# A post-norm decoder trunk on one core: scale rows spread by TensorE at the start, and products grouped by high and low part

## The chip, the cores and the metric

One core of a Trainium2 chip runs the whole program. The time is device microseconds (us) of one execution; several executions are timed, and their median is given. A profile of one further execution shows every instruction on the engines: TensorE (PE, with its weight loads as PEld), the vector engine (DVE), ScalarE (ACT), GpSimd (POOL) and the queue engine (SP). ScalarE's and GpSimd's own DMA issues are shown as ACTq and POOLq.

## The reference

Two layers over 256 tokens of 1024 features, in float32, after one norm of the input (cut to what matters):

```python
h = _layer_norm(x, ln_in_g, ln_in_b)
for l in range(DEPTH):                                   # DEPTH = 2
    mix = _hybrid_mixer(h, positions, w_in[l], ...)      # three attention branches, gates, w_out
    h = _layer_norm(ALPHA * h + mix, ln1_g[l], ln1_b[l])
    ffn = _conv_gated_mlp(h, w_up[l], conv_w[l], conv_b[l], w_down[l])
    h = _layer_norm(ALPHA * h + ffn, ln2_g[l], ln2_b[l])

def _layer_norm(x, g, b):
    mu = jnp.mean(xf, axis=-1, keepdims=True)
    var = jnp.mean(jnp.square(xf - mu), axis=-1, keepdims=True)
    y = (xf - mu) * lax.rsqrt(var + LN_EPS) * g + b
```

The mixer begins with one projection of `h`, whose first 512 columns here are `bq`, the queries of the sparse branch. They are turned by rotary sines and cosines of the positions.

## The kernel before

The 256 tokens are two blocks of 128 (`tb` 0 and 1), one token on each partition. The residual `h` is four tiles of 128 x 512 (`h00`, `h01` for the first block, `h10`, `h11` for the second). A norm (`ln_tail`, `ln_apply`, `ln_stats`) takes statistics on the vector engine, computes the reciprocal deviation `rs` by a power on GpSimd, and applies scale and shift in four steps, two for each half: subtract the mean and multiply by the scale row, then multiply by `rs` and add the shift row. The scale row `lng` and the shift row `lnb` stand on all partitions, loaded as a broadcast. TensorE then transposes each half (four transposes of 128 x 128 into one PSUM bank), ScalarE copies the bank to a rounded high part `hTh`, and the vector engine subtracts to get the low part `hTl`.

Weights are split in the same way. The class `Stream` loads 512 KB chunks on the sync queue into seven buffers (`raw`), and `split` makes from each 128 x 512 item a high part (ScalarE) and a low part (vector engine, or GpSimd where `lo` says so), in 16 buffers `hl0`, `hl1`, and so on. A product of activations and weights is three TensorE instructions: high by high, low activations by high weights, high activations by low weights:

```python
    def mm3(o, lh, ll, rh, rl, start, stop):
        mm(o, lh, rh, start, False)
        mm(o, ll, rh, False, False)
        mm(o, lh, rl, False, stop)
```

A unit with 1024 input features and 512 columns has 8 k tiles, so 24 instructions for a token block. Behind a norm (`unit_x_tbfirst` for `bq` in each layer, and the first pair of the MLP) the first block's 24 go before the second's. The weight items `hl0` to `hl7` are those of `bq` in the first layer; `hl8` and on belong to the next unit, of 332 columns.

The order of every engine is written out as the program is built. Side work (norm tails, attention, rotary) lives in `Tasks` as generators; each `T.tick()` between the steps of the main products takes one step of each and may `refill` one weight split. `Clocks` keeps rough times of the engines, used only to decide that order. On the chip each engine runs its own list strictly in order.

The start of the program (from the comment `constants and first loads`, and again from `program`) sends the loads, normalizes the first block, then the second, and computes the rotary tables in `rotary_tables`: fifteen small operations on GpSimd (`posf`, `ang`, `rn`, `red`), then on ScalarE a load of the Sin table, sine `sn16`, cosine `cc16`, and a load of the table in use before, then copies on GpSimd.

Of the kernel before, what the change touches and what calls it, by code (L numbers as in the profile page):

```python
# [18 lines left out]
P = 128  # L19
D = 1024  # L20
# [14 lines left out]
# halves of the features before a norm  # L35
# [5 lines left out]
# columns of the constant array  # L41
# [32 lines left out]
def stream_plan():  # L74
    """Per layer: (name, first k tile, k tiles, columns) of each chunk in the order of use,
    and the pairs of the MLP whose down products follow a pair's up products."""
# [32 lines left out]
class Stream:  # L109
    """Weights: DMA of 512 KB chunks, each split into float32r high and low parts."""  # L110
# [62 lines left out]
    def refill(self, lo=None):  # L173
        """split one more item, unless the vector engine is behind and enough items are ready"""
# [12 lines left out]
class Clocks:  # L187
    """Rough times of the engines, kept while the program is written down: they only decide
    where in the engines' orders the side work is put."""
# [54 lines left out]
class Tasks:  # L244
    """Side work in pieces, put between the steps of the main products."""
# [40 lines left out]
def tile_hybrid(ctx: ExitStack, tc: tile.TileContext, a: dict, out: bass.AP):  # L286
# [71 lines left out]
    lng = hp.tile([P, D], F32, name="lng0", tag="lng")  # L358
    lnb = hp.tile([P, D], F32, name="lnb0", tag="lnb")
    ident = cpool.tile([P, P], F32, name="ident")  # L360
    sc.dma_start(ident, a["cst"][:, C_ID:C_ID + P])
# [4 lines left out]
    for q in range(2):  # L366
        bc_load(lng[:, 512 * q:512 * q + 512], a["ln_in_g"], 512, 512 * q, nc.sync)
        bc_load(lnb[:, 512 * q:512 * q + 512], a["ln_in_b"], 512, 512 * q, nc.sync)
    W.dma()
    W.dma()  # L370
    for q in range(2):
        nc.sync.dma_start(h[1][q], xv[:, 1, 512 * q:512 * q + 512])
    nc.sync.dma_start(cst[:, C_TRI:C_INVF], a["cst"][:, C_TRI:C_INVF])
    for _ in range(RAW_BUFS - 2):
        W.dma()
# [18 lines left out]
    mhalf = cpool.tile([P, 8], F32, name="mhalf")  # L394
    ve.memset(ones, 1.0)
# [7 lines left out]
    # rotary tables: cos|cos and -sin|sin for 16 and for 8 frequencies  # L403
# [10 lines left out]
    def rotary_tables():  # L414
        """sin and cos of the angles, reduced to [-pi, pi] in three steps"""
# [26 lines left out]
    def lambdas():  # L442
        """minus lambda of the differential attention, on every partition, and its scaled gains"""
# [22 lines left out]
    def ln_half(tb, q, st, bank=None, cols=(0, 512), slot=None):  # L466
        """residual of one half of the features (or a part of it), and its statistics"""
# [5 lines left out]
    def ln_stats(st):  # L473
        """mean and reciprocal deviation"""
# [6 lines left out]

    def ln_apply(tb, st, g, b):
        mu, rs = ln_stats(st)
        for q in range(2):
            y, gq, bq = h[tb][q], g[:, 512 * q:512 * q + 512], b[:, 512 * q:512 * q + 512]
            ve.scalar_tensor_tensor(y, y, mu, gq, ALU.subtract, ALU.mult)
            ve.scalar_tensor_tensor(y, y, rs, bq, ALU.mult, ALU.add)
# [12 lines left out]
    def last_norm0(st, g, b, half_done):  # L500
        """the last norm of the first tokens, spread over the engines"""
# [23 lines left out]
    def ln_tail(tb, st, hT, g, b, flag):  # L525
        """normalise, then transpose into hT"""
# [14 lines left out]
    def unit_x(lhs, kts, ncols):  # L541
        """out[tb] = [token, column]: x stationary, weights moving"""
# [10 lines left out]
    def unit_x_tbfirst(lhs, kts, ncols, ready=None):  # L553
        bk = [acc(), acc()]
        ws = []
        for tb in range(2):
            if ready is not None:
                T.until(lambda: tb in ready)
            for k in range(kts):
                if tb == 0:  # L560
                    ws.append(W.take())
                lh, ll = lhs(k, tb)
                mm3(bk[tb][:, :ncols], lh, ll, ws[k][:, 0, :ncols], ws[k][:, 1, :ncols], k == 0, k == kts - 1)
                if tb == 1:
                    W.free()
                T.tick()
# [708 lines left out]
```

## Time and profile before

| | |
|---|---|
| median of 3 runs | 938.44 us (937.15 to 938.46) |
| profiled execution, its own time: span from first to last instruction | 936.7 us |
| TensorE busy | 905.9 us (97%) |
| vector engine busy | 655.4 us (70%) |
| ScalarE busy | 514.3 us (55%) |
| GpSimd busy | 46.6 us (5%) |
| mean DMA rate | 172 GB/s |

The page gives the profiled execution by its span, which lies 1.74 us below the median of the runs. All instructions carry one line (L238, the recording helper), so the tiles' names tell them apart: `acc` and `att` are PSUM banks, `hl` is a split weight, `raw` a loaded one, `mv` mean and variance, `bst` the statistics, `kbT` the keys of one branch. In a row of the timeline `x2` stands for two instructions merged, and the time in brackets is the engine's idle time ahead of it.

### The profile page before, as it was taken

The page shows a single profiled execution, that of the slowest core. Times are in us where ns is not written, and L with a number is a line of the kernel's source. Part 1 is how long each engine was busy: PE and PEld are TensorE (multiplying, and loading weights), DVE is VectorE, ACT ScalarE, POOL GpSimd, SP SyncE. Part 2 cuts the span into 40 slices and gives each one's busy share as a digit, 9 for nine tenths or more (in the row PEclk, how much of TensorE's full clock was granted, in tenths as well). Part 3 has the DMA queues.
Part 4 walks back from the last instruction along what each step waited for, and adds up shares of the span by engine and source line. Part 5 has one row for each costly group of instructions (what it writes and reads, how often), then busy time and mean ns, then how long its engine had stood idle before and what let it go on. Part 6 is the DMA issues. An engine that isn't in the chain of part 4 may idle for free.

```text
span 936.7 us, 14398 instructions
## 1 busy us (share of the span) xinstructions
PE 905.9 (97%) x5306; PEld 791.9 (85%) x5306; DVE 655.4 (70%) x1270; ACT 514.3 (55%) x1008; POOL 46.6 (5%) x62
## 2 busy tenths in 40 slices
PE   4998999999999999999999999999999999999995
PEld 3876897888888999999988788888888799999994
DVE  6788657657668766666788975665667785766755
ACT  4665567555536655555456565765555375655541
POOL 5000010002000000000010000100110100000001
PEclk9999999999999999999999999999999999999998
DMA  8833427555535755565345343736665286565501
GB/s 305 274 118 113 135 91 260 188 200 185 180 132 211 240 186 191 169 197 191 115 155 174 115 147 111 255 112 206 190 196 179 76 305 200 176 193 192 177 8 45
DMA packets 46535, 161.45 MB, mean 172 GB/s; under 512 B 5696, under 2 KB 6208, under 8 KB 46464
## 3 DMA queue, kind: packets, MB, share of 16 engines
q1 hardware_dynamic: 44208, 154.94, 50.3%
q0 software_dynamic: 1408, 4.98, 1.7%
q8 instruction: 41, 0.67, 0.3%
q10 hardware_dynamic: 848, 0.60, 0.2%
q14 instruction: 30, 0.25, 0.1%
HBM read 159.46 MB, written 1.05 MB: 171 GB/s over the span
## 4 chain that ended last, share of the span: by engine, by line
PE 68%; issue 21%; DVE 7%; DMA 1%; POOL 1%; ACT 1%; SPq 0%; DVEq 0%; POOLq 0%; ACTq 0%
PE acc L238 48%; PE att L238 20%; DVE h L238 2%; DVE s L238 2%; DVE hl L238 1%; POOL rs L238 1%; DVE mx L238 1%; DMA raw<-in_w_dram 1%; DMA lnb<-in_ln_in_b_dram 1%; DVE bst L238 0%; DVE mv L238 0%; ACT h L238 0%; ACT p L238 0%; POOL hl L238 0%; DVE rv L238 0%
## 5 line engine op out<-in xcount | busy, mean ns | idle before, releaser
L238 DVE TENSOR_TENSOR hl<-raw,hl 128x512 fp32r<-128x512 f32 (+1 forms) x581 | 389.1, 695 | 189.6 <-ACT hl L238 188.1
L238 ACT ACTIVATE hl<-raw 128x512 fp32r<-128x512 f32 (+1 forms) x584 | 348.2, 624 | 192.0 <-PE att L238 94.6
L238 PE MATMUL acc<-hl,hTh 128*128 128x512 f32 (+1 forms) x896 | 287.8, 393 | 3.3 <-DVE hl L238 2.0
L238 PE MATMUL att<-hTh,hl 128*128 128x256 f32 x1280 | 231.5, 283 | 0.0
L238 PEld LDWEIGHTS att<-hTh,hl 128*128 128x128 f32 x1280 | 200.8, 192 | 1.4
L238 PEld LDWEIGHTS acc<-hl,hTh 128*128 128x128 f32 x896 | 168.9, 190 | 38.5 <-DVE hl L238 2.7
L238 PE MATMUL att<-hTl,hl 128*128 128x256 f32 x640 | 181.1, 283 | 0.0
L238 PE MATMUL acc<-hl,hTl 128*128 128x512 f32 (+1 forms) x448 | 174.1, 389 | 1.8 <-DVE hTl L238 1.8
L238 PE MATMUL acc<-hl,act 128*128 128x512 f32 x528 | 123.4, 390 | 0.0
L238 PEld LDWEIGHTS att<-hTl,hl 128*128 128x128 f32 x640 | 122.8, 192 | 0.0
L238 PEld LDWEIGHTS acc<-hl,act 128*128 128x128 f32 x528 | 97.9, 188 | 19.5
L238 PEld LDWEIGHTS acc<-hl,hTl 128*128 128x128 f32 x448 | 85.2, 190 | 17.8 <-DVE hTl L238 2.8
L238 PE MATMUL acc<-hl,oT 128*128 128x512 f32 x288 | 68.1, 391 | 0.0
L238 PEld LDWEIGHTS acc<-hl,oT 128*128 128x128 f32 x288 | 53.8, 188 | 11.0
L238 DVE SCALAR_TENSOR_TENSOR cv<-att,convp,cv 128x255 f32<-128x255 f32 x88 | 40.4, 480 | 15.6 <-ACT cv L238 14.0
L238 PE MATMUL acc<-hTh,hl 128*128 128x256 f32 x256 | 47.2, 286 | 0.0
L238 PE MATMUL acc<-hl,mT 128*128 128x512 f32 x192 | 45.4, 392 | 0.0
L238 ACT ACTIVATE hTh<-att 128x512 fp32r<-128x512 f32 x16 | 9.6, 598 | 58.9 <-PE att L238 58.9
L238 PEld LDWEIGHTS acc<-hl,mT 128*128 128x128 f32 x192 | 35.6, 188 | 7.1
L238 PEld LDWEIGHTS acc<-hTh,hl 128*128 128x128 f32 x256 | 39.9, 191 | 1.5 <-issue 1.3
L238 PE MATMUL acc<-hTl,hl 128*128 128x256 f32 x128 | 36.2, 283 | 0.0
L238 POOL TENSOR_TENSOR rs<-mv,mhalf 128x1 f32<-128x1 f32 x10 | 9.0, 904 | 482.2 <-DVE mv L238 482.2
(160 smaller groups left out, 696.0 us busy)
## 6 DMA issues: line engine op xcount, KB each, us to landing
raw<-in_w_dram SPq DMA_DIRECT2D x284, 512.0 KB, 4.3
raw<-in_w_dram SPq DMA_DIRECT2D x8, 332.0 KB, 4.1
lng<-in_ln_g_dram POOLq DMA_DIRECT2D x4, 512.0 KB, 4.2
lnb<-in_ln_b_dram POOLq DMA_DIRECT2D x4, 512.0 KB, 6.6
h<-in_x_dram SPq DMA_DIRECT2D x4, 256.0 KB, 4.6
lng<-in_ln_in_g_dram SPq DMA_DIRECT2D x2, 256.0 KB, 5.3
lnb<-in_ln_in_b_dram SPq DMA_DIRECT2D x2, 256.0 KB, 5.6
wu<-in_w_ukv_dram POOLq DMA_DIRECT2D x2, 256.0 KB, 3.0
```

What stands on the lines that cost most here:

```text
L238: f(*args, **kw)
```

## The change

1. The broadcasts of the first norm's scale and shift rows are gone. One row of 1024 each is loaded to one partition, first on ScalarE's queue, and four float32 products with a stationary row of ones spread the halves over all partitions, into two `acc` and two `att` banks, which the norm reads in place of `lng` and `lnb` until both blocks are through. Four bfloat16 products of a constant tile (`spin`) into a bank that is not read go ahead of them.
2. The first weight chunk is loaded ahead of the second block of `x`, and three more behind it.
3. `hl0` and `hl1` are split while the first block's norm is under way; after that five splits, with GpSimd taking the low parts of `hl2`, `hl3`, `hl4` and `hl6`. The rotary tables are started after these splits, where they had been started before the second block's norm.
4. Behind a norm, products go in groups of four k tiles: the four high by high, then the four with the low activations, then the four with the low weights (`mm3_group`). All ticks of a group fall into its last part. This holds for `bq` in both layers and for the first pair of the MLP in both.

The remaining lines of the diff only take away comments and pass `g` and `b` as two halves.

```diff
-    lng = hp.tile([P, D], F32, name="lng0", tag="lng")
-    lnb = hp.tile([P, D], F32, name="lnb0", tag="lnb")
     ident = cpool.tile([P, P], F32, name="ident")
+    gbr = [hp.tile([P, D], F32, name=f"{n}0", tag=n) for n in ("lng", "lnb")]
+    sc.dma_start(gbr[0][0:1, :], a["ln_in_g"].unsqueeze(0))
+    sc.dma_start(gbr[1][0:1, :], a["ln_in_b"].unsqueeze(0))
...
     for q in range(2):
         nc.sync.dma_start(h[0][q], xv[:, 0, 512 * q:512 * q + 512])
-    for q in range(2):
-        bc_load(lng[:, 512 * q:512 * q + 512], a["ln_in_g"], 512, 512 * q, nc.sync)
-        bc_load(lnb[:, 512 * q:512 * q + 512], a["ln_in_b"], 512, 512 * q, nc.sync)
-    W.dma()
     W.dma()
     for q in range(2):
         nc.sync.dma_start(h[1][q], xv[:, 1, 512 * q:512 * q + 512])
+    for _ in range(3):
+        W.dma()
     nc.sync.dma_start(cst[:, C_TRI:C_INVF], a["cst"][:, C_TRI:C_INVF])
-    for _ in range(RAW_BUFS - 2):
+    for _ in range(RAW_BUFS - 4):
         W.dma()
...
+    spin = t4([P, 512], BF16, n="spin")
+    ve.memset(spin, 1.0)
...
+    def mm3_group(o, ls, ws, first, last):
+
+        n = len(ls)
+        for i, (lh, ll) in enumerate(ls):
+            mm(o, lh, ws[i][0], first and i == 0, False)
+        for i, (lh, ll) in enumerate(ls):
+            mm(o, ll, ws[i][0], False, False)
+        for i, (lh, ll) in enumerate(ls):
+            mm(o, lh, ws[i][1], False, last and i == n - 1)
+            T.tick()
...
-            for k in range(kts):
+            for k in range(0, kts, 4):
                 if tb == 0:
-                    ws.append(W.take())
-                lh, ll = lhs(k, tb)
-                mm3(bk[tb][:, :ncols], lh, ll, ws[k][:, 0, :ncols], ws[k][:, 1, :ncols], k == 0, k == kts - 1)
+                    ws += [W.take() for _ in range(4)]
+                mm3_group(bk[tb][:, :ncols], [lhs(i, tb) for i in range(k, k + 4)],
+                          [(w[:, 0, :ncols], w[:, 1, :ncols]) for w in ws[k:k + 4]], k == 0, k + 4 == kts)
                 if tb == 1:
-                    W.free()
-                T.tick()
+                    W.free(4)
...
+    T.att += 3
+    idle = attp.tile([P, 512], F32, name=nm("att"), tag="att")
+    for _ in range(4):
+        mm(idle, spin[:, 0:P], spin, True)
+    gb = [[acc(), acc()], [attp.tile([P, 512], F32, name=nm("att"), tag="att") for _ in range(2)]]
+    for q in range(2):
+        for i in range(2):
+            mm(gb[q][i], ones[0:1, :], gbr[i][0:1, 512 * q:512 * q + 512], True)
+    T.att -= 1
+    gain, bias = [gb[q][0] for q in range(2)], [gb[q][1] for q in range(2)]
...
-    T.add(ln_tail(0, sts[0], hT, lng, lnb, hflag))
+    T.add(ln_tail(0, sts[0], hT, gain, bias, hflag))
     T.tick()
+    W.split()
+    W.split()
+    T.until(lambda: 0 in hflag)
+    for q in range(2):
+        ln_half(1, q, sts[1])
+    T.add(ln_tail(1, sts[1], hT, gain, bias, hflag))
+    W.low = LOW
+    for i in range(5):
+        W.refill((gp, gp, gp, ve, gp)[i])
+        T.tick()
     tables = rotary_tables()
     next(tables)
-    T.until(lambda: 0 in hflag)
-    for i in range(4):
-        W.refill(ve)
-    for q in range(2):
-        ln_half(1, q, sts[1])
-    T.add(ln_tail(1, sts[1], hT, lng, lnb, hflag))
-    W.low = LOW
-    for i in range(4):
-        W.refill((gp, gp, ve, gp)[i])
-        T.tick()
     T.add(tables)
```

The orders of three engines at the start, row by row. In a name the first number is the tile's own (`hl7` is the eighth weight item), the last a count of the program.

GpSimd, from the end of the rotary angles on. Before, all fifteen operations of the angles stand directly behind the first norm's power, and the first row here is their last:

```order
L238 TENSOR_TENSOR red_142<-red_142,rn_141 128x32
L238 TENSOR_TENSOR hl4_209<-raw2_115,hl4_209 128x512
L238 TENSOR_TENSOR rs_10_215<-mv_9_212,mhalf_135 128x1
L238 TENSOR_TENSOR hl5_221<-raw2_115,hl5_221 128x512
L238 TENSOR_TENSOR hl7_229<-raw3_117,hl7_229 128x512
```

After the change, from the first norm's power on:

```order
L238 TENSOR_TENSOR rs_12_169<-mv_11_166,mhalf_133 128x1
L238 TENSOR_TENSOR hl2_199<-raw1_110,hl2_199 128x512
L238 TENSOR_TENSOR rs_16_205<-mv_15_202,mhalf_133 128x1
L238 TENSOR_TENSOR hl3_211<-raw1_110,hl3_211 128x512
L238 TENSOR_TENSOR hl4_216<-raw2_112,hl4_216 128x512
L238 TENSOR_TENSOR hl6_224<-raw3_114,hl6_224 128x512
L238 CAST posf_139<-posi_95 128x2
L238 TENSOR_SCALAR ang_140<-cst_94,posf_139 128x16 x2
```

The fifteen operations of the angles have moved behind the second norm's power and three low parts.

ScalarE, around the Sin table (`ACT_TABLE_LOAD`). Before:

```order
L238 ACTIVATE hl6_226<-raw3_117 128x512
L238 ACTIVATE hl7_229<-raw3_117 128x512
L238 ACT_TABLE_LOAD
L238 ACTIVATE sn16_144<-ang_140 128x2x16
L238 ACTIVATE cc16_143<-red_142,half_pi_134 128x2x16
L238 ACT_TABLE_LOAD
L238 ACTIVATE hTh_1_147<-att_14_272 128x4x128
```

After the change:

```order
L238 ACTIVATE hl6_224<-raw3_114 128x512
L238 ACTIVATE hTh_7_160<-att_20_262 128x4x128
L238 ACTIVATE hTh_7_160<-att_21_269 128x4x128
L238 ACT_TABLE_LOAD
L238 ACTIVATE sn16_144<-ang_140 128x2x16
L238 ACTIVATE cc16_143<-red_142,half_pi_132 128x2x16
L238 ACT_TABLE_LOAD
L238 ACTIVATE hl7_286<-raw3_114 128x512
```

The second block's two `hTh` now stand ahead of the Sin, and `hl7`, the last item of `bq`, behind it.

TensorE, around the second block's transposes (`h10`, `h11`). Before, with 18 products of the first block ahead of the first row:

```order
L238 MATMUL att_14_272<-ident_98,h10_92 128x128 x4
L238 MATMUL acc_12_243<-hl6_226,hTh_1_147 128x512
L238 MATMUL acc_12_243<-hl6_226,hTl_2_148 128x512
L238 MATMUL acc_12_243<-hl6_226,hTh_1_147 128x512
L238 MATMUL att_15_285<-ident_98,h11_93 128x128 x4
L238 MATMUL acc_12_243<-hl7_229,hTh_1_147 128x512
```

After the change, with 8 products ahead of the first row:

```order
L238 MATMUL acc_18_251<-hl0_175,hTh_7_160 128x512
L238 MATMUL att_20_262<-ident_96,h10_92 128x128 x4
L238 MATMUL att_21_269<-ident_96,h11_93 128x128 x4
L238 MATMUL acc_18_251<-hl1_178,hTh_7_160 128x512
L238 MATMUL acc_18_251<-hl2_199,hTh_7_160 128x512
L238 MATMUL acc_18_251<-hl3_211,hTh_7_160 128x512
L238 MATMUL acc_18_251<-hl4_216,hTh_7_160 128x512
L238 MATMUL acc_18_251<-hl5_219,hTh_7_160 128x512
L238 MATMUL acc_18_251<-hl6_224,hTh_7_160 128x512
L238 MATMUL acc_18_251<-hl7_286,hTh_7_160 128x512
L238 MATMUL acc_18_251<-hl4_216,hTl_8_161 128x512
```

The transposes come after 9 of the first block's products, and `hl7` is used three instructions behind `hl4`, ahead of the low activations. At the three later norms both pairs of transposes come after 21 products; before, 18 came ahead of the first and 21 ahead of the second. Nothing else moves on TensorE.

## Rows read from the trace of the kernel before

**Rows 1.** The page, part 1: busy time, share of the span, instructions.

```profile
PE 905.9 (97%) x5306; PEld 791.9 (85%) x5306; DVE 655.4 (70%) x1270; ACT 514.3 (55%) x1008; POOL 46.6 (5%) x62
```

**Rows 2.** Busy time by stretch: PE, PEld, DVE, ACT, POOL, clock, DMA, GB/s.

```profile
0.00:24.00 24.00, 11.44 (x39) 8.00 (x40) 16.84 (x31) 11.01 (x18) 13.51 (x31) 1.00 0.82 299
24.00:48.00 24.00, 24.00 (x123) 21.03 (x122) 18.37 (x49) 16.11 (x37) 1.39 (x2) 0.93 0.78 266
48.00:140.00 92.00, 88.98 (x553) 75.80 (x552) 68.55 (x199) 51.19 (x138) 3.68 (x5) 1.00 0.35 115
```

**Rows 3.** Timeline (start us, duration us, instruction), vector engine, first block's norm.

```profile
3.66 1.32 DVE L238 BATCH_NORM_STATS2 bst<-h 128x6 f32<-128x512 f32 x2 [2.65 <-DMA h<-in_x_dram]
...
9.50 0.75 DVE L238 SCALAR_TENSOR_TENSOR h<-h,rs,lnb 128x512 f32<-128x512 f32 x1
```

**Rows 4.** Chain that ended last: start us, duration us, what.

```profile
2.10 5.79 DMA lnb<-in_ln_in_b_dram
```

**Rows 5.** Timeline, TensorE, first products.

```profile
12.62 0.80 PE L238 MATMUL acc<-hl,hTh 128*128 128x512 f32 x1 [1.21 <-ACT hl L238]
...
16.20 1.05 PE L238 MATMUL acc<-hl,hTh 128*128 128x512 f32 x2
...
17.48 0.64 PE L238 MATMUL acc<-hl,hTh 128*128 128x512 f32 x2
```

**Rows 6.** Timeline, TensorE, last transposes and end of the first projection.

```profile
23.18 0.60 PE L238 MATMUL att<-ident,h 128*128 128x128 f32 x4
...
30.48 0.61 PE L238 MATMUL acc<-hl,hTh 128*128 128x512 f32 x2
...
31.16 0.54 PE L238 MATMUL acc<-hl,hTh 128*128 128x512 f32 x2
```

**Rows 7.** DMA issues of the first 3.66 us: count, size, median us to landing.

```profile
h<-in_x_dram SPq DMA_DIRECT2D x2, 256.0 KB, 3.0
```

**Rows 8.** Timeline, TensorE, float32 products of another stage.

```profile
86.16 1.03 PE L238 MATMUL att<-kbT,t 128*128 128x256 f32 x4
87.02 0.38 PE L238 MATMUL att<-sb,negid 128*128 128x512 bf16 x1
```

**Rows 9.** The page, part 5: busy us, mean ns of one | idle before.

```profile
L238 DVE TENSOR_TENSOR hl<-raw,hl 128x512 fp32r<-128x512 f32 (+1 forms) x581 | 389.1, 695 | 189.6 <-ACT hl L238 188.1
L238 ACT ACTIVATE hl<-raw 128x512 fp32r<-128x512 f32 (+1 forms) x584 | 348.2, 624 | 192.0 <-PE att L238 94.6
```

**Rows 10.** Timeline, GpSimd: the powers, first and last operations of the angles.

```profile
5.49 0.55 POOL L238 TENSOR_TENSOR rs<-mv,mhalf 128x1 f32<-128x1 f32 x1 [5.06 <-DVE mv L238]
6.00 0.18 POOL L238 CAST posf<-posi 128x2 f32<-128x2 int32 x1
...
10.82 0.29 POOL L238 TENSOR_SCALAR red<-rn 128x32 f32<-128x32 f32 x1
...
12.46 0.25 POOL L238 TENSOR_TENSOR red<-red,rn 128x32 f32<-128x32 f32 x1
...
16.89 1.01 POOL L238 TENSOR_TENSOR rs<-mv,mhalf 128x1 f32<-128x1 f32 x1 [0.15 <-DVE mv L238]
```

**Rows 11.** Instructions on tile hl, 0 to 24 us: ns min/median/max, starts.

```profile
L238 POOL TENSOR_TENSOR hl<-raw,hl x3: 1277/1291/1733, 15.5 to 19.1; 128x512 fp32r<-128x512 f32 x3
```

**Rows 12.** Timeline, ScalarE, cosine and the table load behind it.

```profile
18.66 0.30 ACT L238 ACTIVATE cc<-red,half_pi 128x32 f32<-128x32 f32 x1
...
18.98 1.28 ACT L238 ACT_TABLE_LOAD   x1
...
20.46 0.60 ACT L238 ACTIVATE hTh<-att 128x512 fp32r<-128x512 f32 x1 [0.20 <-PE att L238]
```

**Rows 13.** Busy time by stretch, as in rows 2, inside the first projection.

```profile
24.34:27.75 3.41, 3.41 (x10) 2.65 (x9) 3.32 (x9) 3.41 (x10) 0.00 (x0) 0.50 0.77 197
```

**Rows 14.** Timeline, TensorE and vector engine, norm behind the first mixer.

```profile
283.75 0.50 PE L238 MATMUL acc<-hl,hTl 128*128 128x512 f32 x1 [0.61 <-DVE hTl L238]
...
288.61 0.75 DVE L238 SCALAR_TENSOR_TENSOR h<-h,rs,lnb 128x512 f32<-128x512 f32 x1
```

More of the change, by code (lines that the diff above doesn't have):

```diff
@@ L480, in ln_stats, with halves @@
         return mv[:, 0:1], rs
+    def halves(t):
+        return [t[:, 0:512], t[:, 512:1024]]
     def ln_apply(tb, st, g, b):
@@ L484, in ln_apply @@
         for q in range(2):
-            y, gq, bq = h[tb][q], g[:, 512 * q:512 * q + 512], b[:, 512 * q:512 * q + 512]
+            y, gq, bq = h[tb][q], g[q], b[q]
             ve.scalar_tensor_tensor(y, y, mu, gq, ALU.subtract, ALU.mult)
@@ L1065, in layer @@
                 ln_half(tb, nh, st, ob[nh][tb], (c0, c1), i)
-            T.add(ln_tail(tb, st, hT1, lng, lnb, flag1))
+            T.add(ln_tail(tb, st, hT1, halves(lng), halves(lnb), flag1))
         acts = {}
@@ L1084, in layer @@
             bk = acc()
-            for k in range(KD):
+            ts = slice(tb * P, (tb + 1) * P)
+            for k in range(0, KD, 4):
                 if tb == 0:
-                    ws.append(W.take())
-                ts = slice(tb * P, (tb + 1) * P)
-                mm3(bk, hT1[0][:, k, ts], hT1[1][:, k, ts], ws[k][:, 0, :], ws[k][:, 1, :], k == 0, k == KD - 1)
+                    ws += [W.take() for _ in range(4)]
+                mm3_group(bk, [(hT1[0][:, i, ts], hT1[1][:, i, ts]) for i in range(k, k + 4)],
+                          [(w[:, 0, :], w[:, 1, :]) for w in ws[k:k + 4]], k == 0, k + 4 == KD)
                 if tb:
-                    W.free()
-                T.tick()
+                    W.free(4)
             u = t2([P, 512], n="up0")
@@ L1178, in layer @@
             if l < DEPTH - 1:
-                T.add(ln_tail(tb, st, hT2, lng, lnb, flag2))
+                T.add(ln_tail(tb, st, hT2, halves(lng), halves(lnb), flag2))
             elif tb == 0:
@@ L1193, in tile_hybrid @@
     W.low = -1
-    T.add(ln_tail(0, sts[0], hT, lng, lnb, hflag))
+    T.add(ln_tail(0, sts[0], hT, gain, bias, hflag))
     T.tick()
+    W.split()
[8 more added lines that the diff above has]
+        T.tick()
     tables = rotary_tables()
     next(tables)
-    T.until(lambda: 0 in hflag)
-    for i in range(4):
-        W.refill(ve)
-    for q in range(2):
-        ln_half(1, q, sts[1])
-    T.add(ln_tail(1, sts[1], hT, lng, lnb, hflag))
-    W.low = LOW
-    for i in range(4):
-        W.refill((gp, gp, ve, gp)[i])
-        T.tick()
     T.add(tables)
@@ L1210, in tile_hybrid, with release_gb @@
     masks()
+    def release_gb():
+        while len(hflag) < 2:
+            yield
+        T.att -= 2
+    T.add(release_gb())
     def task_lambdas():
```

## The prediction

> **What bounds the kernel now.** I read the busy times first: TensorE works for 905.9 of 936.7 us [rows 1], so a change is worth what it adds to or takes from TensorE's 30.8 us of idle time and from its clock. The table by stages then says where the idle time lies: 12.6 us in the first 24 us, none from 24 to 48, 3.0 us between 48 and 140 [rows 2]. With no idle time behind it, whatever moves the end of the first projection (the 48 products of `bq`) moves the end of the program. That end is the figure I follow.
>
> The timeline of the start is a chain. The vector engine has the first tokens' statistics at 4.98 us and ends their norm at 10.25 [rows 3]; in between the chain of waits has 5.79 us of the load of `lnb`, issued at 2.10 [rows 4]. TensorE begins the products at 12.62 us; two cost 1.05 us at 16.20 and 0.64 at 17.48 [rows 5], so it begins at the lower of its two clocks. The last product of `bq` starts at 31.16 us; a product costs 0.227 us there, three in the 0.68 us from 30.48 [rows 6]. `bq` ends at 31.4 us.
>
> **First tokens' norm.** The 256 KB broadcasts go, and TensorE spreads two rows. The first loads of 256 KB land 3.0 us after their issue and are in use from 3.66 us [rows 3, 7]; the row of 4 KB goes out first on ScalarE's queue, and I take 3.3 us for its landing. The four spreads are float32: two float32 products of 256 columns go from 86.16 to 87.02 us, so one of 512 columns takes 0.86 us at full clock and 1.72 at half [rows 8]. All at full clock they end at 6.7 us, all at half at 10.2. The four `spin` products start at about 1.2 us, and TensorE needed the work from 12.62 to 17.48 us to get its full clock [rows 5]; 4.9 us after 1.2 is 6.1. By then 1.6 spreads are done, the other 2.4 take 2.0 us: 8.1 us. The norm's last step of 0.75 us stands behind the last spread: 8.1 + 0.1 + 0.75 = 8.95, against 10.25 [rows 3]. That gains 1.3 us, with bounds of a gain of 2.7 and a loss of 0.8.
>
> **The second tokens' norm** follows on the vector engine. Two low parts of weights now come ahead of the two of `hT` (four times 0.695 us [rows 9], 2.8 us), then the statistics, 1.32 [rows 3]: 13.1 us. GpSimd's power begins 0.51 us behind the statistics and takes 0.55 to 1.01 us [rows 3, 10]; I take its end at 14.2. Three more steps of 0.75 follow, and the last four transposes start at 16.4 and take 0.60 us: 17.0, where the trace has 23.18 for their start [rows 6]. So far this looks like a large gain.
>
> **What is moved behind it.** GpSimd computed the rotary angles from 6.00 to 12.71 us [rows 10], ahead of its three low parts. Now they stand behind all three and behind the second norm's power. ScalarE loads the Sin table, computes sine and cosine and loads the other table again, with the last weight tile of `bq`, `hl7`, queued behind; before, all eight tiles went ahead of the Sin. So `hl7` waits for GpSimd:
> - three low parts from 14.2 us, at the median of 1.29 us each: 18.1 us. The dearest was 1.73, which makes 1.3 us more for three [rows 11].
> - the angles: 6.71 us from first to last, part of it waiting for a constant and beside the norm. From 10.82 to 12.46 us five operations come 0.33 us apart [rows 10], which makes 5.0 us for all fifteen. The stretch ahead will be quieter than the first; I take 5.4: 23.5 us.
> - ScalarE: cosine 0.30 and table load 1.28 [rows 12], then the high part of `hl7`, 0.62 [rows 9]: 25.7 us. TensorE takes it at 25.8.
>
> The table load is a place to weigh. In the trace the load at 18.98 us takes 1.28, and the next activation starts at 20.46, after 0.20 us of waiting for TensorE [rows 12], so I use 1.28 alone. The Trainium skill (ScalarE: Activation LUTs, What ACT_TABLE_LOAD costs) puts a drain of about 1.38 us on top of every switch to a different set; by it the sum would come out 1.4 us later. The trace disagrees: 0.2 us is all that stands between that load and the next activation.
>
> **TensorE behind `hl7`.** In the new order the first block's second group asks for the high parts of `hl4` to `hl7` in a row. After 17.0 us six products are free to go (three with low weights, then `hl4`, `hl5`, `hl6`), 1.4 us at full clock and 2.7 at half; at 18.4 to 19.7 us TensorE stands, and waits until 25.8. Then 33 products remain, 9 of the first block and 24 of the second: 33 x 0.227 = 7.5 us. After six idle microseconds the clock will be down. The trace has 3.41 us at granted clock 0.50 in the middle of `bq` [rows 13], 1.7 us lost; the first start had 4.9 us at half [rows 5], 2.4 us lost. So long a stop is nearer to the first start, so 2.4. `bq` ends at 25.8 + 7.5 + 2.4 = 35.7 us instead of 31.4: **4.3 us later**.
>
> **The later norms** (three: after the first layer's mixer and MLP, after the second mixer). The new order fills the wait for `hTl`, 0.61 us at 283.75 [rows 14]. But 21 products stand ahead of the other block's last transposes, before as now, and those are released by the vector engine, whose order ahead of them is the same: its last step ends at 289.36 [rows 14]. TensorE arrives earlier and waits longer there; 27 products follow in both. I cost this edit at nothing, with the vector engine's norm as its cover; without that, three products a norm, 0.68 us, would come off, 2.0 in all.
>
> **Loads.** The sync queue loses 1 MB of broadcasts ahead of the weights, and seven raw buffers can fill while TensorE waits: zero. The smaller moves (a split later, four buffers freed at once) have 16 split buffers as cover: zero; if that cover went, it would be one split, 0.69 us, at each of four places.
>
> **Sum.** 936.7 + 4.3 = 941.0 us of span. The median of the runs stands 1.74 us above that span, so 938.44 + 4.3 = **942.7 us**. Ends of the unknowns: spreads all at full clock (-1.4), power 0.55 (-0.1), angles 5.0 (-0.4), clock loss 1.7 (-0.7) give +1.7; spreads all at half (+2.1), power 1.01 (+0.4), angles 6.7 (+1.3), dear low parts (+1.3) give +9.4, if all came together.
>
> **Rivals.**
> - **TensorE is not held (faster).** Were `hl7` there when TensorE comes, `bq` would end at 17.0 + 39 x 0.227 + 2.4 = 28.3 us, 3.1 us early: 935.3 us. It decides at about 19 us: the chain through GpSimd would have to be over 6 us shorter. For it: spans on GpSimd are rough, by the profile's own word. Against it: three low parts, the angles and the rest on ScalarE are 11.5 us behind a power that can hardly end before 13.
> - **The delay is absorbed (no change).** TensorE idles 3.0 us between 48 and 140 us [rows 2]. If what it waits for there did not move with `bq`, 3.0 of the 4.3 would vanish: 939.7 us. Against it: the selection and softmax it waits for work on these same projections.
> - **The later norms pay.** If the vector engine came 0.7 us earlier to those transposes, 2.0 us would come back: 940.7 us. Against it: nothing is taken from its queue ahead of them.
> - **A table switch costs a drain too**, 1.4 us before `hl7`: 944.1 us. The 0.2 us of [rows 12] speak against it. This is the rule of the page of the Trainium skill named above, ScalarE: Activation LUTs.
>
> **How the numbers follow.** Forecast 0.72, not held 0.08, absorbed 0.07, later norms 0.06, drain 0.07. A measurement of this kernel can tell about 0.2%, 1.9 us, from no change. Only the first rival is faster (0.08); the absorbed one is within 0.2% (0.07); the rest is slower (0.85). The range is 940.1 (+1.7) to 945.6 (+7.2, since the late ends will not all meet); it leaves out the first two rivals and a small tail of the forecast.
>
> **What would show it.** In the changed profile: four spreads of 0.9 to 1.7 us from about 3.3 us; the first tokens' last transposes near 9 us, the second's near 16.4; the angles on GpSimd from 18 to 23.5 us; one wait of TensorE of 6 to 7 us for ScalarE's `hl7`, ending near 25.8; a stretch at clock 0.50 around it; the first product of 332 columns near 35.7. At the later norms the wait for `hTl` gone and one of about 1 us for the vector engine in its place. I am wrong if `hl7` is ready before 20 us, if the angles end before 19 us, or if the waits between 48 and 140 us shrink by some 3 us.

## The result and the profile after

The changed kernel takes **945.37 us** (median of 4 runs, 944.97 to 946.11) against 938.45 us: a ratio of 1.0079 (95% interval 1.0067 to 1.0092), 6.9 us slower. Forecast were 942.7 us, 940.1 to 945.6. The direction and the mechanism are in the trace as forecast; the size is not. The median lies 0.2 us inside the upper end of the range; the ratio, applied to the 938.44 us that the forecast starts from, gives 945.9 us, just above it.

The page, part 1 (busy us, share, instructions), beside [rows 1]:

```profile
PE 914.2 (97%) x5318; PEld 794.5 (84%) x5318; DVE 655.0 (69%) x1270; ACT 514.9 (55%) x1008; POOL 45.7 (5%) x63
```

The span is 944.3 us, 7.6 more; TensorE's idle time has barely moved (30.1 us), its busy time has grown by 8.3. By stretch, with the columns of [rows 2]:

```profile
0.00:24.00 24.00, 16.77 (x43) 7.96 (x43) 15.70 (x30) 8.71 (x13) 9.77 (x21) 0.99 0.77 257
24.00:48.00 24.00, 20.38 (x97) 18.02 (x98) 13.87 (x27) 16.48 (x36) 2.77 (x12) 0.80 0.70 234
48.00:140.00 92.00, 88.96 (x527) 74.72 (x526) 70.09 (x209) 49.09 (x124) 1.91 (x3) 1.00 0.37 119
```

The start is busier because `spin` and the spreads count as work. The loss shows in the second row: 3.6 us idle where there was no idle time, and a granted clock of 0.80 for 0.93. (The same wait also fills the last 3.5 us of the first row.) The third row is as before, so nothing is absorbed there.

TensorE's timeline at the start, the rows that answer to [rows 5]; a float32 spread is two instructions here:

```profile
1.45 1.89 PE L238 MATMUL att<-spin 128*128 128x512 bf16 x4 [1.45 <-DVE spin L238]
3.27 2.07 PE L238 MATMUL acc<-lng,ones 1*128 1x512 f32 x2
...
8.55 1.91 PE L238 MATMUL att<-lnb,ones 1*128 1x512 f32 x2
...
12.19 1.22 PE L238 MATMUL acc<-hl,hTh 128*128 128x512 f32 x2
...
14.48 1.09 PE L238 MATMUL acc<-hl,hTl 128*128 128x512 f32 x4
15.40 0.39 PE L238 MATMUL acc<-hl,hTh 128*128 128x512 f32 x1
```

From 5.13 us the spreads start 1.71 us apart, the length at half clock in [rows 8]: all four run at the lower level, although TensorE has worked since 1.45. The products of the four low parts at 14.48 us (0.92 us up to the next row) are the first at full speed. The vector engine's last step of the first norm waits for the last of them, where [rows 3] has its start at 9.50:

```profile
10.49 0.75 DVE L238 SCALAR_TENSOR_TENSOR h<-h,rs,att 128x512 f32<-128x512 f32 x1 [0.96 <-PE att L238]
```

GpSimd, the second norm's power, the three low parts, the first and the last operation of the angles ([rows 10] has those two at 6.00 and 12.46):

```profile
15.48 0.56 POOL L238 TENSOR_TENSOR rs<-mv,mhalf 128x1 f32<-128x1 f32 x1 [0.54 <-DVE mv L238]
16.00 4.20 POOL L238 TENSOR_TENSOR hl<-raw,hl 128x512 fp32r<-128x512 f32 x3
20.15 0.18 POOL L238 CAST posf<-posi 128x2 f32<-128x2 int32 x1
...
25.02 0.25 POOL L238 TENSOR_TENSOR red<-red,rn 128x32 f32<-128x32 f32 x1
```

ScalarE behind it, as in [rows 12]. The first of the nine high parts is `hl7`, and it starts at the end of the load (25.65 + 1.28 = 26.93), with no drain:

```profile
25.31 0.32 ACT L238 ACTIVATE cc<-red,half_pi 128x32 f32<-128x32 f32 x1 [0.73 <-POOL red L238]
25.65 1.28 ACT L238 ACT_TABLE_LOAD   x1
26.94 3.59 ACT L238 ACTIVATE hl<-raw 128x512 fp32r<-128x512 f32 x9
```

TensorE's hold, and the first visible product of the next block, of 332 columns (31.53 us before):

```profile
27.62 0.80 PE L238 MATMUL acc<-hl,hTh 128*128 128x512 f32 x1 [7.12 <-ACT hl L238]
...
38.25 0.31 PE L238 MATMUL acc<-hl,hTl 128*128 128x332 f32 x1
```

And the half-clock stretch around the hold, where [rows 13] has one of 3.41 us:

```profile
23.54:33.78 10.24, 6.16 (x15) 4.86 (x16) 4.01 (x9) 5.42 (x12) 3.15 (x13) 0.50 0.61 170
```

So the next block begins 6.7 us late, and 6.7 it stays: the first product behind the first mixer's norm is at 289.38 instead of 282.65 ([rows 14]), the 72 products of the last TensorE stage begin at 917.21 instead of 910.39. At the later norms the wait for `hTl` is gone and one for the vector engine stands in its place, as forecast; from that first product to the end of the unit it is 13.47 us before and 13.48 now:

```profile
296.23 0.63 PE L238 MATMUL att<-ident,h 128*128 128x128 f32 x4 [0.82 <-DVE h L238]
```

Some 0.8 us more of the span are lost behind the last stage (27.09 us from the start of its 72 products to the end, 26.31 before); part of them is explained with e10 below.

### The profile page after: what moved, and what is told of

The parts are those of the page before. It is cut to its first block, busy times and chain, and to the rows that moved or that the text cites. A ratio compares the mean times of both kernels' runs of the same rounds, so it can differ in the third digit from the quotient of the medians.

```text
span 944.3 us, 14436 instructions
## 1 busy us (share of the span) xinstructions
PE 914.2 (97%) x5318; PEld 794.5 (84%) x5318; DVE 655.0 (69%) x1270; ACT 514.9 (55%) x1008; POOL 45.7 (5%) x63
## 4 chain that ended last, share of the span: by engine, by line
PE 69%; issue 21%; DVE 6%; POOL 2%; ACT 1%; DVEq 0%; POOLq 0%; ACTq 0%
PE acc L238 48%; PE att L238 21%; DVE h L238 2%; DVE s L238 2%; DVE hl L238 1%; DVE mx L238 1%; POOL rs L238 1%; POOL hl L238 1%; DVE bst L238 0%; DVE mv L238 0%; POOL ang L238 0%; ACT hl L238 0%; ACT h L238 0%; ACT p L238 0%; POOL red L238 0%
## 5 line engine op out<-in xcount | busy, mean ns | idle before, releaser
L238 PE MATMUL acc<-hl,hTh 128*128 128x512 f32 (+1 forms) x896 | 279.4, 392 | 7.3 <-ACT hl L238 7.3
L238 PE MATMUL acc<-hl,hTl 128*128 128x512 f32 (+1 forms) x448 | 165.7, 388 | 0.0
L238 ACT ACTIVATE p<-att,smx 128x128 f32<-128x128 f32 (+1 forms) x48 | 19.5, 425 | 23.5 <-DVE smx L238 23.5
```

Source lines behind the costliest of these rows:

```text
L238: f(*args, **kw)
```

## Experiments

Each kernel is the change with one edit, unless it says otherwise. "Next block" is the first visible product (of `hTl`) of the 512-column block behind the 332-column one: 39.71 us before, 46.42 in the change. The ratio is to the kernel before, with its 95% interval.

| kernel | next block, us | median, us | ratio |
|---|---|---|---|
| the change | 46.42 | 945.37 | 1.0079 (1.0067 to 1.0092) |
| e1_hl7_first | 38.40 | 937.85 | 0.9997 (0.9988 to 1.0006) |
| e2_angles_early | 42.46 | 942.58 | 1.0048 (1.0035 to 1.0061) |
| e3_both_moves | 38.18 | 939.84 | 1.0021 (1.0012 to 1.003) |
| e4_group_only | 38.49 | 937.45 | 0.9991 (0.9982 to 0.9999) |
| e5_no_groups | 45.48 | 944.83 | 1.0072 (1.0059 to 1.0084) |
| e6_broadcast | 47.29 | 946.38 | 1.009 (1.0076 to 1.0104) |
| e7_splits_before_tables | 40.93 | 940.39 | 1.0025 (1.0016 to 1.0034) |
| e8_splits_broadcast | 41.36 | 940.37 | 1.0024 (1.0014 to 1.0034) |
| e9_copy_first | 36.44 | 935.95 | 0.9976 (0.9966 to 0.9985) |
| e10_copy_first_pad | 36.43 | 935.56 | 0.997 (0.9959 to 0.9982) |
| e11_one_pass_spread | 44.80 | 945.26 | 1.0083 (1.0069 to 1.0096) |
| e12_best_one_pass | 35.90 | 934.8 | 0.997 (0.9959 to 0.9981) |

**e1_hl7_first**: is it the hold on `hl7`? One more split ahead of the Sin table.

```diff
-    for i in range(5):
-        W.refill((gp, gp, gp, ve, gp)[i])
+    for i in range(6):
+        W.refill((gp, gp, gp, ve, gp, ve)[i])
```

> The changed kernel with a sixth split ahead of the rotary tables, so that hl7's high part stands ahead of the Sin table on ScalarE; nothing else moves. Theory A (the 7.1 us in which TensorE stands for hl7 are the loss): after the second transposes, 18.85 us in the changed kernel, 39 products of 0.227 us follow without a stop, bq ends at 27.7 to 28.5 instead of 38.1, and the time is 935 to 936 us, 9.5 to 10.5 below the changed kernel and 2.5 to 3.5 below the kernel before. Theory B (the hold only moves on: the next weight item, hl8, is now the one behind the Sin table and the angles, and TensorE stands for it): bq ends early, but the first product of 332 columns waits for hl8 and the time is above 938. Theory C (the loss comes from the slow spreads and the groups, and the wait only covers it): 943 us or more.

One split moved takes away 7.5 us: 937.85 against 945.37. The hold of 7.1 us is gone, and with it the half clock around it (granted clock 1.00 from 13 to 48 us); the 332-column block begins at 28.28 us. That the hold is the cause is shown. Theory A's 935 to 936 us is not reached, though the next block comes 1.3 us earlier than before: some of that goes at the end of the program (see e10), and the rest of the gain hoped for goes into a new stop. TensorE waits for the transposes behind the rotation of `bq` (the row names ScalarE, but the rotation's last step on the vector engine ends only at 33.97 us).

```profile
34.12 1.06 PE L238 MATMUL att<-ident,t 128*128 128x128 f32 x8 [1.51 <-ACT hl L238]
```

**e2_angles_early**: `hl7` left where it is, the angles back ahead of the splits.

```diff
+    tables = rotary_tables()
+    next(tables)
     W.split()
     W.split()
...
-    tables = rotary_tables()
-    next(tables)
```

> The changed kernel with GpSimd's angles started directly behind the first norm's power, as in the kernel before; the Sin table and hl7 behind it stay where the change put them on ScalarE. Theory A: sine and cosine no longer wait, so hl7 follows the second block's high parts (19.76 us) by two table loads, sine and cosine, 3.2 us, and its own 0.6: TensorE takes hl7 at about 23.6 instead of 27.6 us, bq ends 4 to 6 us earlier than in the changed kernel, time 939 to 941.5 us. Theory C (spreads and groups are the loss): 944 us or more.

A hold remains, 2.1 us, and two half-clock stretches of 3.4 us each (18.93 to 22.34, 25.76 to 29.17). So having the angles behind GpSimd's low parts makes 5 of the hold's 7 us; ending them earlier shortens the hold but doesn't end it. The time misses the 939 to 941.5 us expected: `hl7` now waits for the second norm, whose power stands behind the angles and a low part (its last transposes start at 19.41 us, 0.9 later), and then for the two table loads with sine and cosine between them.

```profile
24.88 0.50 PE L238 MATMUL acc<-hl,hTh 128*128 128x512 f32 x1 [2.08 <-ACT hl L238]
```

**e3_both_moves**: both edits.

> Both moves of the first two runs together: hl7 ahead of the Sin table and the angles early. Theory A: bq ends at 27.7 to 28.5 us as with hl7 alone, and hl8 is ready by 24 us, so the time is that of the first run or up to 1 us less, 934.5 to 936 us. Theory B would show here: if the first run stands for hl8 and this one does not, the difference of the two is that wait.

No hold, and in the profiled run the next block comes earlier than in e1. But its eleven runs go from 937.66 to 940.64 us, and the profiled one is the shortest: it has one half-clock stretch (18.67 to 22.08 us) and a mean granted clock of 0.995. Seven of the others have 0.992, and lie from 939.66 to 940.64. The expectation missed this, and one profile of this kernel isn't its median. The three runs left, 938.92 to 939.64 us at 0.995 and 0.997, say that the clock is not all of it; what the rest is stays open.

**e4_group_only**: the kernel before, with the products of both places in groups, and nothing else of the change.

```diff
-            for k in range(kts):
...
-                mm3(bk[tb][:, :ncols], lh, ll, ws[k][:, 0, :ncols], ws[k][:, 1, :ncols], k == 0, k == kts - 1)
+            for k in range(0, kts, 4):
...
+                mm3_group(bk[tb][:, :ncols], [lhs(i, tb) for i in range(k, k + 4)],
+                          [(w[:, 0, :ncols], w[:, 1, :ncols]) for w in ws[k:k + 4]], k == 0, k + 4 == kts)
```

> The kernel before with the grouped products alone (spread, loads, splits and angles as before). My prediction: the groups are worth nothing at the three later norms, since the vector engine's norm releases the other block's transposes, and at the start hl0 to hl7 are all ahead of the Sin table: 938.4 us, within 0.7 of the kernel before. Rival (the groups pay at each norm): 2 us below it, 936.4. Rival (the groups cost, since the high parts of four items are wanted at once): 1 us or more above it.

0.8 us faster, just outside no change and a little more than the 0.7 allowed for. The gain lies in the start (next block 1.2 us early); at the later norms the wait moves as in the change, and none of the 2.0 us of the third rival comes back.

**e5_no_groups**: the change with k by k again at both places (the edit of e4 undone).

> The change with the products behind a norm k by k again instead of in groups. Theory A (the hold on the eighth split of bq sets the end, and the group puts 33 instead of 27 products behind it): the hold stays, ends at 27 to 28 us, and 6 products of 0.23 us fewer are left behind it: 944.0 us (943.4 to 944.6). Rival B (the group is worth here what it was worth alone, 0.8 us, because of the later norms or the first waits): 946.2 us. Rival C (neither): 945.4 us.

Between the theories: the next block is 0.9 us earlier, the median 0.5, and the intervals of the two ratios overlap. The hold ends later here, at 28.61 us, because two copies of the second norm now stand ahead of `hl7` on ScalarE (26.96, 1.09 us); the six products fewer behind it more than make up for it. The groups are not what the change loses.

**e6_broadcast**: the scale rows loaded to all partitions again, no spread and no `spin`.

```diff
-    sc.dma_start(gbr[0][0:1, :], a["ln_in_g"].unsqueeze(0))
...
+    for q in range(2):
+        bc_load(lng[:, 512 * q:512 * q + 512], a["ln_in_g"], 512, 512 * q, nc.sync)
...
-            mm(gb[q][i], ones[0:1, :], gbr[i][0:1, 512 * q:512 * q + 512], True)
```

> The change with the first norm's scale rows loaded to all partitions by DMA as before, no products of ones and no spin; loads, splits and groups as changed. Theory A (the half-clock spreads delay the first norm by 1.0 us, and through the second norm, the low parts and the angles the eighth split): first norm ends at 10.2 to 10.4 instead of 11.2 us, the hold ends 1.0 us earlier, 944.4 us (943.9 to 944.9). Rival B (the spreads are off the path, the hold is set by the raw weights or the angles alone): 945.4 us. Rival C (without the early products TensorE's granted clock rises later, as before, where it was full from 17.5 us instead of 13.3 us, and the first block's products run at half): 945.5 to 947 us.

Rival C by the total, but not by its reason. The first norm does end 1.2 us earlier (9.32 + 0.75), and TensorE's first rows at full speed come late, at 18.02 us (four transposes in 0.66 us, at 10.13 in 1.11; in the change it was 14.48 us, not the 13.3 of the expectation). But TensorE then waits for the transposes and for `hl7` all the same, and the hold ends at 29.01, 1.4 us later, for something that nobody had expected. The vector engine's timeline in the second norm, with gain and bias in SBUF, and GpSimd's beside it (the second norm's power, the three low parts, the last operation of the angles):

```profile
16.21 1.75 DVE L238 SCALAR_TENSOR_TENSOR h<-h,rs,lnb 128x512 f32<-128x512 f32 x1 [0.45 <-POOL rs L238]
17.89 1.75 DVE L238 SCALAR_TENSOR_TENSOR h<-h,mv,lng 128x512 f32<-128x512 f32 x1
19.68 1.63 DVE L238 SCALAR_TENSOR_TENSOR h<-h,rs,lnb 128x512 f32<-128x512 f32 x1
```

```profile
15.18 1.00 POOL L238 TENSOR_TENSOR rs<-mv,mhalf 128x1 f32<-128x1 f32 x1 [0.30 <-DVE mv L238]
16.15 4.62 POOL L238 TENSOR_TENSOR hl<-raw,hl 128x512 fp32r<-128x512 f32 x3
...
26.41 0.25 POOL L238 TENSOR_TENSOR red<-red,rn 128x32 f32<-128x32 f32 x1
```

The same steps beside the same low parts, with gain and bias in PSUM (the change):

```profile
16.16 0.75 DVE L238 SCALAR_TENSOR_TENSOR h<-h,rs,acc 128x512 f32<-128x512 f32 x1
16.82 0.74 DVE L238 SCALAR_TENSOR_TENSOR h<-h,mv,att 128x512 f32<-128x512 f32 x1
17.60 0.75 DVE L238 SCALAR_TENSOR_TENSOR h<-h,rs,att 128x512 f32<-128x512 f32 x1
```

So the spreads cost the vector engine 1.2 us in the first norm and save it 2.9 us in the second (three steps of 1.75, 1.75 and 1.63 for three of 0.75). The kernel before has two such steps too, 1.78 and 1.77 us at 17.93 and 19.63. The hold, however, follows GpSimd, and there the sum is this: the power starts 0.3 us earlier than in the change (most of the 1.2 us is gone by then, since behind the broadcasts the first weights come late: ScalarE's first high part starts at 10.32 us for 8.39); then the power takes 0.44 us more, the low parts 0.42, and the fifteen operations of the angles 0.82 (20.72 to 26.66 for 20.15 to 25.27). That is the 1.4 us.

**e7_splits_before_tables**: e1, and five splits of the 332-column block ahead of the tables.

```diff
+    def tables_late():
+        while len(hflag) < 2:
+            yield
+        for _ in range(5):
+            W.refill(ve)
+        yield from tables
-    T.add(tables)
+    T.add(tables_late())
```

> e1 (eighth split ahead of the sine table) with five splits of the 332-column block also ahead of the tables, after the second norm's copies, in the 3.9 us that ACT waits for the angles. Theory A (what e1 lost again, 1.5 us, was the queue of eight splits in front of the copy of bq out of its bank, and so rope's transposes): transposes come without a wait, 936.3 us (935.8 to 936.8). Rival B (the tables come later by the five splits, rope is as late as in e1): 937.8 us. Rival C (a denser start moves a half-clock stretch into it, as in the run with both moves): 938 to 939.5 us.

A miss, above all three ranges: 2.5 us slower than e1. ScalarE's timeline shows that seven more high parts still stand ahead of the copies of `bq`, and the angles end 0.6 us later beside the vector engine's early low parts. TensorE stops for the transposes for 3.0 us, and behind that its clock falls (0.58 in the mean from 35 to 39 us).

```profile
26.82 1.28 ACT L238 ACT_TABLE_LOAD   x1
28.12 3.32 ACT L238 ACTIVATE hl<-raw 128x332 fp32r<-128x332 f32 x7
31.34 1.06 ACT L238 ACTIVATE t<-acc 128x512 f32<-128x512 f32 x2
```

```profile
35.04 1.41 PE L238 MATMUL att<-ident,t 128*128 128x128 f32 x8 [2.99 <-DVE t L238]
```

**e8_splits_broadcast**: e7 with the edit of e6.

> e7 with the scale rows loaded by DMA as before, no spread and no spin. Theory A (the spreads cost 1.0 us of the first norm and give nothing back): 935.3 us, 1.0 below e7. Rival B (the early products bring the full clock 4 us earlier, which e7 keeps and this loses): 937 to 938 us, above e7, with half clock to about 17 us in the trace.

The same time as e7, with neither theory. As in e6 the second norm's steps take 1.75, 1.75 and 1.63 us; its last transposes start at 21.99 us for 18.49, and there is half clock again (0.50 from 22 to 24 us). In exchange TensorE does not stop for rope's transposes. The next block is 0.4 us later than in e7, and the end of the program about as much shorter (its stores are issued 0.44 us apart, see e10).

**e9_copy_first**: e7 with all eight splits of that block early, and none between the tables and the copies.

```diff
-        for _ in range(5):
+        for _ in range(8):
             W.refill(ve)
+        W.hold, W.low = True, -1
...
-        T.add(task_rope_T(evac(bk), 4, 32, 128 ** -0.5, "qbT"))
+        bq = evac(bk)
+        if l == 0:
+            W.hold, W.low = False, LOW
+        T.add(task_rope_T(bq, 4, 32, 128 ** -0.5, "qbT"))
```

> e7 with all eight splits of the 332-column block ahead of the tables, and none between the tables and the copies of bq out of its two banks, so that on ACT the copies stand right behind the table load. Theory A (the stop of 1.5 us in e1 and 3.0 us in e7 for rope's transposes is the queue of eight or seven high parts ahead of these copies): copies by 29.3 us, rope by 30.7 us, TensorE does not stop for the transposes and reaches the next block at 36.9 us, 1.5 us before e1: 936.3 us (935.7 to 936.8). Rival B (the angles, slowed by the vector engine's low parts beside them, set rope's time): transposes still wait by 1 us or more, 937.5 to 940 us. Rival C (a half-clock stretch): 938 us.

As theory A has it, in place and in size: 935.95 us. ScalarE's and TensorE's rows that answer to those of e7 (the transposes start without a wait):

```profile
27.16 1.28 ACT L238 ACT_TABLE_LOAD   x1
28.46 1.09 ACT L238 ACTIVATE t<-acc 128x512 f32<-128x512 f32 x2
```

```profile
32.13 1.06 PE L238 MATMUL att<-ident,t 128*128 128x128 f32 x8
```

**e10_copy_first_pad**: the end of the program. In the change the sync queue's last two stores are issued 0.76 us apart, before 0.45; its DMA view lists an instruction packet in that stretch (the row of queue 14), which before it doesn't, and a store lands 3.3 us after its issue instead of 2.1. Four loads fewer stand on that queue. The change:

```profile
939.21 0.35 SPq L494 DMA_DIRECT2D out_dram<-h  x1
939.97 0.34 SPq L519 DMA_DIRECT2D out_dram<-h  x1
```

```profile
q14 instruction: 1, 0.01, 0.2%
...
out_dram<-h SPq DMA_DIRECT2D x2, 256.0 KB, 3.3
```

e10 is e9 with four tiny loads more on the sync queue at the start:

```diff
+    pad = cpool.tile([1, 64], F32, name="pad")
+    for i in range(4):
+        nc.sync.dma_start(pad[:, 16 * i:16 * i + 16], a["ln_in_g"][0:16].unsqueeze(0))
```

> e9 with four loads of 64 bytes more on the sync queue at the start, into a tile that nothing reads, so that this queue has as many instructions as in the kernel before. Theory A (in the change the packet of instructions that the trace shows between the last two stores of the sync queue costs 0.3 us of issue and some 0.4 us of landing): that packet gone, stores issued 0.45 us apart, 0.7 us below e9: 935.6 us. Rival B (packet and landing have nothing to do with each other or with the count): same as e9 within 0.2 us.

```profile
929.16 0.35 SPq L497 DMA_DIRECT2D out_dram<-h  x1
929.61 0.38 SPq L522 DMA_DIRECT2D out_dram<-h  x1
```

The packet is gone from the end, the stores are 0.45 us apart and land in 2.0, and the time falls by 0.4 us, to the 935.6 expected, at the same next block (e9 lay lower than its forecast, so the step is 0.4 and not 0.7). The other traces bear it out: the packet stands between the last stores, 0.74 to 0.77 us apart, in all eight kernels without four such loads, and in none of the six that have them or the broadcasts (before, e4, e6, e8, e10, e12: 0.44 or 0.45). Why the number of loads decides it stays open. e10 beats both kernels with the reference's full computation: 2.8 us below before, 9.8 below the change.

**e11_one_pass_spread**: the spreads as float32r products, one pass; rows loaded over GpSimd's queue.

```diff
-    sc.dma_start(gbr[0][0:1, :], a["ln_in_g"].unsqueeze(0))
+    gp.dma_start(gbr[0][0:1, :], a["ln_in_g"].unsqueeze(0).bitcast(R32))
...
-            mm(gb[q][i], ones[0:1, :], gbr[i][0:1, 512 * q:512 * q + 512], True)
+            mm(gb[q][i], ones_r, gbr[i][0:1, 512 * q:512 * q + 512], True)
```

> The change with its four spreads as float32r products, one pass over the columns instead of four (the low bits of gain and bias are left out; the two rows are loaded by GpSimd's queue). At half clock a product is then 0.43 us instead of 1.71. Theory A (the first norm's late end, 11.24 us against the 8.95 forecast, is the float32 spreads at half clock, and it is what made the eighth split 1.8 us later than forecast): first norm ends at 8.4 to 8.9 us, TensorE takes the eighth split at 25.0 to 25.9 us, 943.3 us (942.8 to 943.9). Rival B (raw weights, in use from 8.39 us, or ScalarE set the eighth split anyway): first norm earlier, the hold ends within 0.5 us of 27.6, 945.4 us. Rival C (with 5 us less of early products the granted clock rises later and takes the gain): half clock past 14 us, 944.5 to 946 us.

The rows land only at 6.4 us on that queue, so the norm gains 0.9 us instead of 2.5. What it gains, the hold gains one for one (26.73 for 27.62):

```profile
9.60 0.75 DVE L238 SCALAR_TENSOR_TENSOR h<-h,rs,att 128x512 f32<-128x512 f32 x1
```

```profile
26.73 0.79 PE L238 MATMUL acc<-hl,hTh 128*128 128x512 f32 x1 [7.11 <-ACT hl L238]
```

So the first norm's end is at the head of the chain to `hl7`, which speaks against rival B. With a shorter half-clock stretch behind it the next block comes 1.6 us earlier, and so much apart are the two profiled executions (944.53 and 946.11). The median doesn't show it: 945.26 us, with runs from 944.53 (the profiled one) to 946.54 at mean clocks of 0.991 to 0.993. In total the test is inconclusive; 0.9 us is less than the clock moves this kernel's runs.

**e12_best_one_pass**: e10 with the edit of e11.

> e10 with the same one-pass spreads (low bits of gain and bias left out). Theory A (in e10 too the first norm is at the head of the chain): everything to the rope transposes comes 1.5 to 2.5 us earlier, 933.5 us (933.0 to 934.3). Rival B (in e10 the raw weights, in use from 8.4 us, and the angles on GpSimd set the pace): under 0.5 us, 935.3 us. Rival C (the clock rises later): 935.6 us or more, with half clock past 14 us.

Between the theories: next block 0.5 us earlier, 0.8 us in the median, ratios that overlap. The rows land late here too (the second at 7.5 us), and the products of the first block are at half length until 16 us, later than in e10. It leaves low bits out, so e10 stays the version to keep.

## Why the prediction was right and wrong

- **What bounds, and where to follow it: right.** TensorE's shift at the end of `bq` is the shift of everything behind it, 6.7 us at 38 and at 289 us, 6.8 at 917.
- **The mechanism: right.** One hold of TensorE of 7.1 us (6 to 7 forecast), on `hl7`, behind table load, angles and low parts. e1 takes it away by moving one split, and 7.5 us with it.
- **"By then 1.6 spreads are done, the other 2.4 take 2.0 us: 8.1 us": the step that failed.** I gave the start the 4.9 us that lay between TensorE's first product and the full clock in [rows 5]. Here the first full-speed products start at 14.48 us, 13.0 after the first of `spin`, and all four spreads ran at half. I had that bound and put the value nearer to the other one. The first norm ended at 11.24 instead of 8.95, worse than the 10.25 before; the second norm's power at 16.04 (14.2 forecast), the low parts at 20.2 (18.1), the angles at 25.27 (23.5), and TensorE took `hl7` at 27.62 (25.8): 1.8 us of the error. This is read from the chain; e11 bears it out for 0.9 us (first norm and hold both 0.9 earlier), and no run took away the whole delay.
- **The GpSimd terms: right.** Low parts 4.2 us (3.9 forecast), angles 5.1 (5.4); power 0.56.
- **"So long a stop is nearer to the first start, so 2.4": too small by 0.7.** 6.16 us of products ran at half clock, which costs 3.1 us. 1.8 and 0.7 make the 2.4 us between 6.7 and the 4.3 forecast, within rounding. This is the second term of the sum that was mis-sized: it was argued by likeness, with no row for a stop of that length.
- **Later norms, loads, table drain: right.** Zero, zero and not seen. By the drain of about 1.38 us that the Trainium skill gives (ScalarE: Activation LUTs, What ACT_TABLE_LOAD costs), `hl7` would, as an estimate, have started near 28.3 us; the trace disagrees: it started at 26.94, at the load's end.
- **What I left out.** That gain and bias in PSUM keep the vector engine's steps at 0.75 us beside GpSimd. I used 0.75 without a reason and was right by luck: the steps of 1.78 and 1.77 us stood in the trace of before, unread, and with them that norm would have ended some 2 us later in the sum. The total would not have moved, since `hl7` waits for GpSimd; but e6 shows that GpSimd's power, low parts and angles pay for such steps too, and the 0.55 to 1.01 us that I gave the power as an unknown has its likely reason there (1.00 in e6, 0.56 in the change). I also left out the end of the program: 0.3 us of issue and about 0.5 behind it.
- **The rivals.** Absorbed, later norms and drain are excluded by the trace. "Not held" is what e1 makes of the change; the 935.3 us that I gave it came only with e9 (935.95) and e10 (935.56), when the next stop had gone too.
- **The range.** Of the four late ends in the sum one came in full, spreads all at half (+2.1), and one in small part, the low parts (+0.3). The clock loss had no late end at all: 2.4 us was the most that the sum had for it, and it took 3.1. So +7.2 was wide enough for the shift of 6.7 only because it held late ends that did not come.

## What to carry to other kernels

Before work is moved behind other work on an engine off the critical path, follow what it releases through every queue in order: here the angles cost nothing themselves, but one weight tile queued behind the sine on ScalarE held TensorE for 7 us, and moving that one split ahead of the sine again was worth the whole loss. When one stop goes, look for the next in the same queue (e1 to e9: the copies behind the splits). And a clock-dependent price should be taken at its slow end at the start of a program: the products that were to raise the clock themselves ran at half.

## What the hardware showed that was not expected

- **Vector engine and GpSimd.** In the second norm a step with two tensors in SBUF took 1.63 to 1.75 us beside GpSimd's low parts, with one of them in PSUM 0.75 (e6 against the change). The Trainium skill (GPSIMD Engine Reference, Specifications) states that GpSimd shares its SBUF interfaces with the vector engine, and that vector instructions with two SBUF inputs contend there. The traces agree. It goes both ways: GpSimd's power took 1.00 us there and 0.56 here, its three low parts 4.62 and 4.20. And the vector engine does not always pay: in the change its low part of weights begun at 18.26 us, with both inputs in SBUF, took only 0.78, while GpSimd's low part begun at 18.45 took 1.75, for 1.27 of the one before it.
- **Clock at the start.** With `spin` and float32 spreads from 1.45 us on, products ran at half speed until 14.4 us; before, with nothing until 8.86, until 17.4 ([rows 5]), and in e6 past 16.8. So full speed came some 3 us earlier in this trace, too late for the spreads themselves. That the early work is worth those 3 us is not shown: the same start has half-length products until about 16 us in e9, and e4, with no early work, until about 15.8. The column of granted clock doesn't show any of this: it reads 1.00 from 5 to 10 us, where the spreads take their half-clock length. At the start the lengths of products are to be read.
- **The last stores.** Four loads of 64 bytes at the start of a queue took 0.3 us from the time between its last two stores (e10 against e9), with an instruction packet that no longer fell between them.
